# A hybrid decoder layer: the softmax values of one quad joined to the logits of a later quad, and retention's values of a head to the scores of the next

## The chip, the cores and the metric

The kernel runs on one core of a Trainium2 chip. The metric is the device time of one execution in microseconds (us), the median over the runs, lower is better. Four engines matter: TensorE (PE, matmuls; PEld is its weight loads), VectorE (DVE), ScalarE (ACT), and the DMA queues, mostly issued from SyncE (SP).

## What is computed

One layer on 256 tokens of width 2048, in fp32. The reference, cut to the middle part, which the change touches:

```python
x = x + 0.5 * gate1 * swiglu(modulate(rms_norm(x)), w_ffn1_gu, w_ffn1_down)
h = modulate(rms_norm(x))
rq, rk, rv, rg, sq, sk, sv, gl_ret, gl_swa = split(h @ w_in)
# sliding-window attention, 32 query heads over 8 key/value heads of 64, window 128, one sink per head
logits = einsum(q, k) * 64 ** -0.5              # masked to the window
probs = softmax(concat([logits, sink]))[..., :-1]
so = einsum(probs, v)
# retention, 8 heads: q, k of 128, v of 256, chunks of 128
scores = einsum(rotary(rq), rotary(rk)) * decay
ro = einsum(scores, rv) + (what comes over from the chunk before)
ro = silu(rg) * ro * rsqrt(mean(ro * ro) + 1e-6)
merged = sigmoid(gl_ret) * (ro @ w_ret_branch) + sigmoid(gl_swa) * (so @ w_swa_branch)
x = x + gate2 * (merged @ w_out)
x = x + 0.5 * gate3 * swiglu(modulate(rms_norm(x)), w_ffn2_gu, w_ffn2_down)
```

## The kernel before

**The large products.** Every weight is streamed from memory once, as tiles `raw` of 128 x 2048 (four row blocks by 512 columns). A tile is used in two **pieces** of 128 x 1024. For each piece ACT makes the high part `wh` (a cast to a shorter format, L351) and DVE makes the rest `wl = raw - wh` (L353). PE then does 12 matmuls of 512 columns: two row blocks, two halves of the tokens, and three products each (L338 and L339 with `wh`, L341 with `wl`). `wh` and `wl` come from a pool of three buffers each (`wsp`), so ACT can cast a piece only when PE has finished with the piece three before it.

**The work beside them.** The products of the projection `h @ w_in` come in chunks of 512 columns, each of 8 pieces: key and value of the attention, four chunks of its queries (SQ), four of retention's queries and keys (RQ, RK, with a rotation on DVE, L1262 to L1274), four of its values (RV), and so on. After every second piece `gemm` calls `step()`, which advances one generator of the list `side` by one yield. Softmax and retention run there, between the pieces. Rows of the conditioning matrix `w_ada` are summed on DVE as well (L206, four passes per row, at a pace set by `RATE_SOFT` and `RATE_AFTER`). The tile framework decides the order on PE, DVE and ACT from priorities and from its own picture of the timing; each engine then takes its list strictly in that order. SP's order is the order of the code.

**Softmax before.** A **quad** is four query heads that share one key head. `softmax_heads` runs quad g over four steps (parts 0 to 3) and beyond. Part 0, `quad_weights(g)`: a burst of logits on PE (8 matmuls, L1117, contraction of 64, so in 64 x 128 tiles of the array, into two `pd` and two `ps` banks); then on DVE the masked logits (L1125, four), the maximum (L1137, two), small operations (L1139 to L1141); on ACT eight exponentials (L1146); on DVE the sum, its inverse and the scaling (L1150 to L1153). Part 2: ACT takes the result apart into planes (L1167), a DMA of SP turns those of the quad before (L1176). Part 3 of the next quad: DVE puts the turned planes together into `turned_p` (L1188, four copies, `quad_together`). Part 1 two quads later: `quad_values`, a burst of 6 matmuls on PE (L1201, 128 x 64 tiles) into a `ps` bank of its own, copied out at L1205. Both bursts are placed with high priority behind the newest matmul of the big product.

**Retention before.** `retention(h)` makes the scores of head h (L1286, L1289), scales them by the decay on DVE, yields, then does the values (L1299 to L1301), their mean square (ACT) and the scaling, and yields again. A chunk of RV adds two heads to `side`.

Of the kernel before, what the change touches and what calls it, by code (L numbers as in the profile page):

```python
# [9 lines left out]
F32 = mybir.dt.float32  # L10
# [7 lines left out]
P = 128  # L18
S = 256
D = 2048  # L20
DFF = 5632
NT = S // P
# [8 lines left out]
RH, RDK, RDV = 8, 128, 256  # L31
QH, KVH, HD = 32, 8, 64
# [7 lines left out]
C_DEC = C_MASK + 3 * P  # L40
# [37 lines left out]
def layer_kernel(  # L78
# [56 lines left out]
    def a512():  # L135
        return t512()
# [177 lines left out]
    side = []  # L314
# [42 lines left out]
    cast, low, newest = [], [], []  # L357
# [173 lines left out]
    def flat_tile():  # L531

        return flat.tile([P, CH], F32, tag="flat", name=nm("flat"))
# [351 lines left out]
    part = [slot() for _ in range(3)]  # L885
# [212 lines left out]
    QUADS, HQ = QH // 4, 4  # L1098
# [6 lines left out]
    halves = [slice(i * HD, (i + 1) * HD) for i in range(2)]  # L1105
    asked, dec = set(), []

    def quad_weights(g):

        assert g // 2 in asked  # L1110
        late = [side_bank() for _ in range(2)]
        early_q = [bank() for _ in range(2)]
        with tc.issue_after(newest[-1]), tc.high_priority(offset=300):
            for ps, qs, n in ((late, slice(P, S), S), (early_q, slice(0, P), P)):
                for a in range(2):
                    for i, hs in enumerate(halves):
                        nc.tensor.matmul(  # L1117
                            ps[i][:, a * n : (a + 1) * n],
                            qo[hs, 2 * g + a, qs], skt[hs, g, :n], start=True, stop=True,
                        )  # L1120
        by_half = logits.rearrange("p (a i) n -> p a i n", a=2)
        for ps, ns in ((late, slice(P, W3)), (early_q, slice(0, P))):
            n = ns.stop - ns.start
            for i in range(2):
                nc.vector.scalar_tensor_tensor(  # L1125
                    out=by_half[:, :, i, ns],
                    in0=ps[i][:, : 2 * n].rearrange("p (a n) -> p a n", a=2),
                    scalar=HD**-0.5,
                    in1=mask[:, None, ns].broadcast_to([P, 2, n]),
                    op0=ALU.mult,  # L1130
                    op1=ALU.add,
                )
        mx, ng, se, sm = (small(2 * HQ, tag) for tag in ("mx", "ng", "se", "sm"))
        m2, n2, s2 = (v.rearrange("p (t i) -> p t i", t=2) for v in (mx, ng, se))
        parts_of = (logits[:, :, :P], logits[:, :, P:])
        for t, of_t in enumerate(parts_of):
            nc.vector.tensor_reduce(out=m2[:, t, :], in_=of_t, axis=AX.X, op=ALU.max)  # L1137
        sb = sink_b[:, HQ * g : HQ * (g + 1)][:, None, :].broadcast_to([P, 2, HQ])
        nc.vector.tensor_tensor(out=m2, in0=m2, in1=sb, op=ALU.max)  # L1139
        nc.vector.tensor_scalar(out=ng, in0=mx, scalar1=-1.0, scalar2=None, op0=ALU.mult)  # L1140
        nc.vector.tensor_tensor(out=s2, in0=n2, in1=sb, op=ALU.add)  # L1141
        nc.scalar.activation(se, se, AF.Exp)
        for t, of_t in enumerate(parts_of):
            for i in range(HQ):
                z = t * HQ + i
                nc.scalar.activation(  # L1146
                    of_t[:, i, :], of_t[:, i, :], AF.Exp,
                    bias=ng[:, z : z + 1], accum_out=sm[:, z : z + 1],
                )
        nc.vector.tensor_add(sm, sm, se)  # L1150
# [31 lines left out]
    def quad_together(turned):  # L1182

        for a in range(2):
            into = turned_p[:, 2 * a : 2 * a + 2].rearrange("p h b q -> p (h b q)")
            with tc.issue_after(low[-1]):
                for i in range(2):
                    nc.vector.tensor_copy(  # L1188
                        words(into)[:, :, i], turned[a][:, i * 2 * W3 : (i + 1) * 2 * W3]
                    )  # L1190

    def quad_values(g):

        po = bank()
        p4 = po.rearrange("p (a t q) -> p a t q", a=2, t=NT)
        vs = slice(g * HD, (g + 1) * HD)
        heads = turned_p.rearrange("p (a i) b q -> p a i b q", a=2)
        with tc.issue_after(newest[-1]), tc.high_priority(offset=300):
            for t, blk, tv in ((0, 0, 0), (1, 1, 0), (1, 2, 1)):
                for i in (1, 0):  # L1200
                    nc.tensor.matmul(  # L1201
                        p4[halves[i], :, t, :], sv[:, tv, vs], heads[:, :, i, blk, :],
                        start=blk < 2, stop=blk != 1,
                    )
        nc.any.tensor_copy(  # L1205
            qo[:, 2 * g : 2 * g + 2, :].rearrange("p a s -> p (a s)"), po
        )

    def softmax_heads():

        turned = {}
        for at in range(4 * (QUADS + 1) + 2):
            g, part = divmod(at, 4)
            if part == 0 and g < QUADS:
                quad_weights(g)
            if part == 1 and g >= 2:
                quad_values(g - 2)
            if part == 2 and g >= 1:
                turned[g - 1] = quad_turn()
            if part == 2 and g < QUADS:  # L1220
                quad_apart()
            if part == 3 and g >= 1:
                quad_together(turned.pop(g - 1))
                if g == QUADS:
                    dec.append(one.tile([P, D], F32, tag="row", name="dec"))
                    nc.gpsimd.dma_start(dec[0], consts[:, C_DEC:])
            yield
        pace["rate"] = RATE_AFTER
        turns.append(rows_beside())
# [19 lines left out]
    kept = set()  # L1249
# [30 lines left out]

    vo = slot().rearrange("p (t n) -> p t n", t=NT)

    def retention(h):
        assert {(0, h // 4), (1, h // 4)} <= kept
        ps = side_bank()
        nc.tensor.matmul(  # L1286
            ps[:, :S], qk[:, 1, h, :P], qk[:, 0, h, :], start=True, stop=True
        )
        nc.tensor.matmul(  # L1289
            ps[:, S : S + P], qk[:, 1, h, P:], qk[:, 0, h, P:], start=True, stop=True  # L1290
        )
        sc = a512()
        dh = dec[0][:, h * S : (h + 1) * S]
        nc.vector.tensor_mul(sc[:, :S], ps[:, :S], dh)
        nc.vector.tensor_mul(sc[:, S : S + P], ps[:, S : S + P], dh[:, :P])
        yield
        hv = slice(h * RDV, (h + 1) * RDV)
        po = side_bank()
        nc.tensor.matmul(po[:, :RDV], sc[:, :P], vo[:, 0, hv], start=True, stop=True)  # L1299
        nc.tensor.matmul(po[:, RDV:], sc[:, P:S], vo[:, 0, hv], start=True, stop=False)  # L1300
        nc.tensor.matmul(  # L1301
            po[:, RDV:], sc[:, S : S + P], vo[:, 1, hv], start=False, stop=True
        )
        v = small(NT, "rvar")
        junk = a512()
# [19 lines left out]
        yield  # L1325

    for ci in range(4):
        b = in_chunk(O_RV + ci * CH)
        for t in range(NT):
            nc.any.tensor_copy(vo[:, t, ci * CH : (ci + 1) * CH], b[t])  # L1330
        side += [retention(h) for h in (2 * ci, 2 * ci + 1)]

    def gates(p):

# [171 lines left out]
```

## Time and profile before

| what | value |
|---|---|
| median of 3 runs | 2375.23 us (2373.46 to 2377.26) |
| profiled execution | 2376.93 us, of which its span, first to last instruction, is 2375.2 us |
| granted TensorE clock | 0.998 |
| DVE busy | 1702.5 us (72%) |
| ACT busy | 1322.7 us (56%) |
| idle time of PE's matmuls put down to another engine between 880 and 1220 us, where softmax and retention run | 0.7 us |

Softmax begins at 882 us (first logits burst) and its last values burst ends at 1114 us; retention ends at 1209 us. Read a timeline row as: start, length, engine, line, operation, output<-inputs, shape, count, and in brackets the idle time before it with what ended it. Matmuls overlap in the pipeline, so the step from start to start is what one costs, not its length.

### The profile page before, as it was taken

The numbers are of one execution on the slowest core, as the hardware profiler recorded it, in microseconds if no ns is written. First come the engines' busy times: TensorE is split into PE (matmuls) and PEld (weight loads), VectorE is DVE, ScalarE is ACT, GpSimd is POOL, SyncE is SP. The second block draws the span as 40 slices with busy tenths as digits, with TensorE's granted clock in tenths as the row PEclk, the third lists the DMA queues.
The fourth block names the chain that finished last, engine by engine and source line by source line (L and its number), as shares of the span: only waits on it lengthen the run. The fifth ranks groups of instructions, "written<-read, shape, count | busy, mean of one in ns | idle before, by whom it ended". The sixth has DMA issues, their size and how long they took to land.

```text
span 2375.2 us, 28320 instructions
## 1 busy us (share of the span) xinstructions
PE 2342.6 (99%) x10438; PEld 1921.9 (81%) x10438; DVE 1702.5 (72%) x2635; ACT 1322.7 (56%) x1816; POOL 7.7 (0%) x18
## 2 busy tenths in 40 slices
PE   7999999999999999999999999999999999999998
PEld 5788888888788887778888888887888888888886
DVE  6887799788977768976777776677555555555656
ACT  6543456555446568775556564466445455455544
POOL 0000000000000000000000000000000000000000
PEclk9999999999999999999999999999999999999999
DMA  9977789998876787986778887755677777766553
GB/s 358 362 279 274 269 279 355 373 343 315 313 264 242 272 276 237 245 241 237 273 259 298 298 301 279 286 200 184 244 242 240 253 241 254 247 220 204 190 200 124
DMA packets 186028, 627.87 MB, mean 264 GB/s; under 512 B 108769, under 2 KB 109153, under 8 KB 115361
## 3 DMA queue, kind: packets, MB, share of 16 engines
q1 hardware_dynamic: 183810, 615.21, 74.4%
q0 software_dynamic: 1504, 9.81, 1.0%
q8 instruction: 82, 1.34, 0.2%
q10 hardware_dynamic: 576, 1.05, 0.1%
q14 instruction: 56, 0.46, 0.1%
HBM read 597.16 MB, written 4.22 MB: 253 GB/s over the span
## 4 chain that ended last, share of the span: by engine, by line
PE 94%; DVE 2%; DMA 2%; issue 1%; ACT 0%; SPq 0%; DVEq 0%; ACTq 0%
PE pa L341 31%; PE pa L338 31%; PE pa L339 31%; DMA raw<-in_w_ada_dram 1%; DVE wl L353 1%; PE ps L1201 0%; DMA x_sb<-in_x_dram 0%; DVE raw L206 0%; PE pd L1117 0%; DMA raw<-in_w_ffn_gu_dram 0%; DVE slot L206 0%; ACT wh L351 0%; PE ps L817 0%; DVE t L607 0%; PE ps L1117 0%
## 5 line engine op out<-in xcount | busy, mean ns | idle before, releaser
L353 DVE TENSOR_TENSOR wl<-raw,wh 128x1024 fp32r<-128x1024 f32 x794 | 964.6, 1222 | 532.9 <-ACT wh L351 531.1
L351 ACT CAST wh<-raw 128x1024 fp32r<-128x1024 f32 x794 | 833.5, 1053 | 906.1 <-PE pa L339 876.2
L338 PE MATMUL pa<-wh,hh 128*128 128x512 f32 x2192 | 856.4, 392 | 3.3 <-ACT wh L351 3.3
L339 PE MATMUL pa<-wh,hl 128*128 128x512 f32 x2192 | 855.2, 390 | 0.2 <-DVE hl L601 0.2
L341 PE MATMUL pa<-wl,hh 128*128 128x512 f32 x2192 | 779.4, 392 | 1.4 <-DVE wl L353 1.2
L338 PEld LDWEIGHTS pa<-wh,hh 128*128 128x128 f32 x2192 | 411.9, 188 | 92.3 <-ACT wh L351 5.3
L341 PEld LDWEIGHTS pa<-wl,hh 128*128 128x128 f32 x2192 | 410.5, 188 | 90.0 <-DVE wl L353 4.1
L339 PEld LDWEIGHTS pa<-wh,hl 128*128 128x128 f32 x2192 | 412.3, 188 | 85.2 <-DVE hl L601 0.4
L339 PE MATMUL pa<-wh,a 128*128 128x512 f32 x944 | 367.3, 391 | 0.0
L341 PE MATMUL pa<-wl,a 128*128 128x512 f32 x944 | 349.6, 391 | 3.1 <-DVE wl L353 3.1
L338 PE MATMUL pa<-wh,a 128*128 128x512 f32 x944 | 350.6, 391 | 0.0
L206 DVE CUSTOM_DVE_ANT_0 slot<-slot,cact 128x512 f32<-128x512 f32 (+1 forms) x280 | 210.3, 800 | 12.5 <-DMA slot<-in_w_ada_dram 12.5
L341 PEld LDWEIGHTS pa<-wl,a 128*128 128x128 f32 x944 | 177.7, 188 | 40.7 <-DVE wl L353 4.2
L339 PEld LDWEIGHTS pa<-wh,a 128*128 128x128 f32 x944 | 177.6, 188 | 38.4 <-DVE a L387 1.5
L338 PEld LDWEIGHTS pa<-wh,a 128*128 128x128 f32 x944 | 177.6, 188 | 37.0 <-ACT a L386 0.4
L512 ACT COPY slot<-back 128x512 uint16<-128x512 uint16 x140 | 93.4, 766 | 0.0
L206 DVE CUSTOM_DVE_ANT_0 raw<-raw,cact 128x512 f32<-128x512 f32 (+1 forms) x108 | 70.7, 706 | 21.2 <-DMA raw<-in_w_ada_dram 14.9
L206 DVE CUSTOM_DVE_ANT_0 rows_x<-rows_x,cact 128x512 f32<-128x512 f32 x124 | 78.7, 687 | 9.7 <-DMA rows_x<-in_w_ada_dram 9.3
L387 DVE TENSOR_TENSOR a<-slot,a 128x512 fp32r<-128x512 f32 x118 | 80.6, 684 | 0.3
L496 ACT COPY flat<-t 128x512 uint16<-128x512 uint16 x128 | 72.7, 617 | 3.0 <-DVE t L1274 2.6
L386 ACT CAST a<-slot 128x512 fp32r<-128x512 f32 x118 | 72.6, 616 | 0.0
L206 DVE DVE_READ_ACCUMULATOR2_ANT sums<- 128x1 f32 x512 | 42.0, 82 | 0.0
(206 smaller groups left out, 1162.5 us busy)
## 6 DMA issues: line engine op xcount, KB each, us to landing
raw<-in_w_ffn_gu_dram SPq DMA_DIRECT2D x160, 1024.0 KB, 5.2
raw<-in_w_in_dram SPq DMA_DIRECT2D x104, 1024.0 KB, 5.5
raw<-in_w_ffn_down_dram SPq DMA_DIRECT2D x88, 1024.0 KB, 4.8
slot<-in_w_ada_dram SPq DMA_DIRECT2D x83, 1024.0 KB, 7.2
rows_x<-in_w_ada_dram SPq DMA_DIRECT2D x31, 1024.0 KB, 7.4
raw<-in_w_ada_dram SPq DMA_DIRECT2D x26, 1024.0 KB, 5.5
raw<-in_w_ffn_gu_dram SPq DMA_DIRECT2D x32, 512.0 KB, 5.8
raw<-in_w_swa_branch_dram SPq DMA_DIRECT2D x16, 1024.0 KB, 6.0
```

The source lines that it names most:

```text
L206: nc.vector.tensor_tensor_reduce(out=w[:, at], in0=w[:, at], in1=cact[:, at], scale=1.0, scalar=0.0, op0=ALU.mult, op1=ALU.add, accum_out= ...
L338: nc.tensor.matmul(ps, ah[:, j, ts], wh[:, j, :], start=first, stop=False)
L339: nc.tensor.matmul(ps, al[:, j, ts], wh[:, j, :], start=False, stop=False)
L341: nc.tensor.matmul(ps, ah[:, j, ts], wl[:, j, :], start=False, stop=last).ins
L351: cast.append(nc.scalar.copy(hi, src).ins)
L353: low.append(nc.vector.tensor_sub(lo, src, hi.bitcast(F32)).ins)
L386: nc.scalar.copy(hi, v)
L387: nc.vector.tensor_sub(lo, v, hi.bitcast(F32))
L496: nc.scalar.copy(planes[:, i, :], words(src)[:, :, i])
L512: nc.scalar.copy(into[:, :, :, i], held["turned"][:, i])
```

## The change

**Softmax.** The logits of quad g and the values of quad g-3 go into one burst, `quad_burst`, at part 0: first the values, then the logits. The values no longer have a bank of their own: they go into the upper halves of the two `ps` banks whose lower halves take the early logits. They are copied out by two copies in place of one. `quad_together(g-2)` moves from part 3 of a quad to part 1 of the next, that is behind the burst. The generator is three steps longer; `dec`, retention's decay, is loaded one step earlier.

**Retention.** One generator for all heads: the values of head h-1 and the scores of head h in one burst, placed behind the newest matmul with high priority; nine steps in place of sixteen. The values go to a `ps` bank and not to a `pd` bank, the squares' unread output to a `flat` tile.

```diff
-    def quad_weights(g):
-        assert g // 2 in asked
-        late = [side_bank() for _ in range(2)]
-        early_q = [bank() for _ in range(2)]
+    def quad_burst(g, gv):
+        late = [side_bank() for _ in range(2)] if g is not None else None
+        both = [bank() for _ in range(2)]
         with tc.issue_after(newest[-1]), tc.high_priority(offset=300):
...
+            if gv is not None:
+                vs = slice(gv * HD, (gv + 1) * HD)
+                heads = turned_p.rearrange("p (a i) b q -> p a i b q", a=2)
+                for t, blk, tv in ((0, 0, 0), (1, 1, 0), (1, 2, 1)):
+                    for i in (1, 0):
                         nc.tensor.matmul(
+                            both[t][halves[i], S:].rearrange("p (a q) -> p a q", a=2),
+                            sv[:, tv, vs], heads[:, :, i, blk, :],
+                            start=blk < 2, stop=blk != 1,
                         )
+            if g is not None:
...
+                for ps, qs, n in ((late, slice(P, S), S), (both, slice(0, P), P)):
...
+        if gv is not None:
+            for t in range(NT):
+                nc.any.tensor_copy(
+                    qo[:, 2 * gv : 2 * gv + 2, t * P : (t + 1) * P],
+                    both[t][:, S:].rearrange("p (a q) -> p a q", a=2),
+                )
+        if g is not None:
+            quad_weights(g, late, both)
...
-        for at in range(4 * (QUADS + 1) + 2):
+        for at in range(4 * (QUADS + 2) + 1):
             g, part = divmod(at, 4)
-            if part == 0 and g < QUADS:
-                quad_weights(g)
-            if part == 1 and g >= 2:
-                quad_values(g - 2)
-            if part == 2 and g >= 1:
+            if part == 1 and 2 <= g < QUADS + 2:
+                quad_together(turned.pop(g - 2))
+            if part == 0 and (g < QUADS or g >= 3):
+                quad_burst(g if g < QUADS else None, g - 3 if g >= 3 else None)
+            if part == 2 and 1 <= g <= QUADS:
                 turned[g - 1] = quad_turn()
...
-            if part == 3 and g >= 1:
-                quad_together(turned.pop(g - 1))
...
     def retention(h):
-        assert {(0, h // 4), (1, h // 4)} <= kept
-        ps = side_bank()
...
+        g = h if h < RH else None
+        ps, po = side_bank(), bank()
+        with tc.issue_after(newest[-1]), tc.high_priority(offset=300):
+            if h > 0:
+                sc, hv = held_scores.pop(h - 1), slice((h - 1) * RDV, h * RDV)
+                nc.tensor.matmul(po[:, :RDV], sc[:, :P], vo[:, 0, hv], start=True, stop=True)
...
+            if g is not None:
+                assert {(0, h // 4), (1, h // 4)} <= kept
+                nc.tensor.matmul(
+                    ps[:, :S], qk[:, 1, h, :P], qk[:, 0, h, :], start=True, stop=True
+                )
...
+    def retention_heads():
+        for h in range(RH + 1):
+            while h // 2 not in valued and h < RH:
+                yield
+            retention(h)
+            yield
```

How the order moves is shown for quad 3 (its logits are the fourth burst of softmax), whose place in the program is the same in both kernels. Numbers behind a name are buffers and differ between the two programs. On PE, before, the logits of quad 3 stand alone, and the values of quad 1 follow three pieces and more later (not among these rows):

```order
L1117 MATMUL pd_7555<-slot_6204,slot_6366 128x256
L1117 MATMUL pd_7556<-slot_6204,slot_6366 128x256
L1117 MATMUL pd_7555<-slot_6204,slot_6366 128x256
L1117 MATMUL pd_7556<-slot_6204,slot_6366 128x256
L1117 MATMUL ps_7557<-slot_6204,slot_6366 128x128
```

and now the values of quad 0 stand right ahead of them (`soft` holds `turned_p`):

```order
L1118 MATMUL ps_7545<-soft,slot_6204 64x256 x2
L1118 MATMUL ps_7546<-soft,slot_6204 64x256 x4
L1128 MATMUL pd_7543<-slot_6204,slot_6366 128x256
L1128 MATMUL pd_7544<-slot_6204,slot_6366 128x256
L1128 MATMUL pd_7543<-slot_6204,slot_6366 128x256
```

Between this burst and the next PE has 96 matmuls of the big product, 8 pieces, with nothing between them; before, a values burst stood among the 96.

On ACT, before, at quad 3, from the cast of the third piece behind the burst (`wh_7642`) on:

```order
L351 CAST wh_7642<-raw_7640 128x1024
L496 COPY flat_7552<-t_7497 128x512 x2
L496 COPY flat_7629<-t_7504 128x512 x2
L351 CAST wh_7661<-raw_7640 128x1024
L351 CAST wh_7689<-raw_7687 128x1024
L351 CAST wh_7705<-raw_7687 128x1024
L1205 COPY slot_6366<-ps_7632 128x512
L1146 ACTIVATE soft,sm_7574<-soft,ng_7572 128x128 x4
L1146 ACTIVATE soft,sm_7574<-soft,ng_7572 128x256 x4
L1142 ACTIVATE se_7573<-se_7573 128x8
L351 CAST wh_7743<-raw_7741 128x1024
L351 CAST wh_7760<-raw_7741 128x1024
```

and now, again from the third piece on (`wh_7634`; L1134 copies the values out, L1168 is the exponentials):

```order
L351 CAST wh_7634<-raw_7632 128x1024
L496 COPY flat_7540<-t_7485 128x512 x2
L496 COPY flat_7625<-t_7492 128x512 x2
L1134 COPY slot_6366<-ps_7545 128x2x128
L1134 COPY slot_6366<-ps_7546 128x2x128
L351 CAST wh_7653<-raw_7632 128x1024
L1168 ACTIVATE soft,sm_7570<-soft,ng_7568 128x128 x3
L1164 ACTIVATE se_7569<-se_7569 128x8
L1168 ACTIVATE soft,sm_7570<-soft,ng_7568 128x128
L1168 ACTIVATE soft,sm_7570<-soft,ng_7568 128x256 x4
L351 CAST wh_7681<-raw_7679 128x1024
L351 CAST wh_7697<-raw_7679 128x1024
```

The exponentials stood behind the cast of the sixth piece after the burst; they stand behind that of the fourth now. Counted in the same way, quad 2 goes from five to four, and quads 2 to 7 all have four in the changed kernel, as quad 0 has in both.

On DVE, before, at quad 3, from the `wl` of the third piece on:

```order
L353 TENSOR_TENSOR wl_7643<-raw_7640,wh_7642 128x1024
L1125 SCALAR_TENSOR_TENSOR soft<-pd_7555,small_c 128x2x256
L1125 SCALAR_TENSOR_TENSOR soft<-pd_7556,small_c 128x2x256
L1125 SCALAR_TENSOR_TENSOR soft<-ps_7557,small_c 128x2x128
L1125 SCALAR_TENSOR_TENSOR soft<-ps_7558,small_c 128x2x128
L353 TENSOR_TENSOR wl_7662<-raw_7640,wh_7661 128x1024
L1137 TENSOR_REDUCE mx_7571<-soft 128x4 x2
L353 TENSOR_TENSOR wl_7690<-raw_7687,wh_7689 128x1024
L1139 TENSOR_TENSOR mx_7571<-mx_7571,sink_b 128x8
L353 TENSOR_TENSOR wl_7706<-raw_7687,wh_7705 128x1024
L1140 TENSOR_SCALAR ng_7572<-mx_7571 128x8
```

and now (L1210 is `quad_together`, L1147 the masked logits, L1159 the maximum, L1162 `ng`, on which the exponentials wait, L1172 the sum, which waits for them):

```order
L353 TENSOR_TENSOR wl_7635<-raw_7632,wh_7634 128x1024
L1210 COPY soft<-a_7443 128x768 x2
L1210 COPY soft<-a_7444 128x768 x2
L1147 SCALAR_TENSOR_TENSOR soft<-pd_7543,small_c 128x2x256
L1147 SCALAR_TENSOR_TENSOR soft<-pd_7544,small_c 128x2x256
L1147 SCALAR_TENSOR_TENSOR soft<-ps_7545,small_c 128x2x128
L353 TENSOR_TENSOR wl_7654<-raw_7632,wh_7653 128x1024
L1159 TENSOR_REDUCE mx_7567<-soft 128x4 x2
L1161 TENSOR_TENSOR mx_7567<-mx_7567,sink_b 128x8
L1162 TENSOR_SCALAR ng_7568<-mx_7567 128x8
L1163 TENSOR_TENSOR se_7569<-ng_7568,sink_b 128x8
L1172 TENSOR_TENSOR sm_7570<-sm_7570,se_7569 128x8
```

The copies of `quad_together` have come in ahead of the masked logits, and no `wl` stands any more between the maximum and the sum.

More of the change, by code (lines that the diff above doesn't have):

```diff
@@ L1190, in quad_together @@
                     )
[L1192 to L1207, printed above, removed]
     def softmax_heads():
         turned = {}
-        for at in range(4 * (QUADS + 1) + 2):
+        for at in range(4 * (QUADS + 2) + 1):
             g, part = divmod(at, 4)
-            if part == 0 and g < QUADS:
-                quad_weights(g)
-            if part == 1 and g >= 2:
-                quad_values(g - 2)
-            if part == 2 and g >= 1:
+            if part == 1 and 2 <= g < QUADS + 2:
[3 more added lines that the diff above has]
+            if part == 2 and 1 <= g <= QUADS:
                 turned[g - 1] = quad_turn()
@@ L1221, in softmax_heads @@
                 quad_apart()
-            if part == 3 and g >= 1:
-                quad_together(turned.pop(g - 1))
-                if g == QUADS:
-                    dec.append(one.tile([P, D], F32, tag="row", name="dec"))
-                    nc.gpsimd.dma_start(dec[0], consts[:, C_DEC:])
+            if part == 2 and g == QUADS:
+                dec.append(one.tile([P, D], F32, tag="row", name="dec"))
+                nc.gpsimd.dma_start(dec[0], consts[:, C_DEC:])
             yield
@@ L1281, in layer_kernel @@
     vo = slot().rearrange("p (t n) -> p t n", t=NT)
+    held_scores = {}
     def retention(h):
-        assert {(0, h // 4), (1, h // 4)} <= kept
-        ps = side_bank()
[L1286 to L1303, printed above, removed]
+        g = h if h < RH else None
+        ps, po = side_bank(), bank()
@@ new lines, in retention @@
+        with tc.issue_after(newest[-1]), tc.high_priority(offset=300):
+            if h > 0:
+                sc, hv = held_scores.pop(h - 1), slice((h - 1) * RDV, h * RDV)
+                nc.tensor.matmul(po[:, :RDV], sc[:, :P], vo[:, 0, hv], start=True, stop=True)
+                nc.tensor.matmul(
+                    po[:, RDV:], sc[:, P:S], vo[:, 0, hv], start=True, stop=False
+                )
+                nc.tensor.matmul(
+                    po[:, RDV:], sc[:, S : S + P], vo[:, 1, hv], start=False, stop=True
+                )
+            if g is not None:
+                assert {(0, h // 4), (1, h // 4)} <= kept
+                nc.tensor.matmul(
+                    ps[:, :S], qk[:, 1, h, :P], qk[:, 0, h, :], start=True, stop=True
+                )
+                nc.tensor.matmul(
+                    ps[:, S : S + P], qk[:, 1, h, P:], qk[:, 0, h, P:], start=True, stop=True
+                )
@@ L1304, in retention @@
+        if g is not None:
+            sc = held_scores[h] = a512()
+            dh = dec[0][:, h * S : (h + 1) * S]
+            nc.vector.tensor_mul(sc[:, :S], ps[:, :S], dh)
+            nc.vector.tensor_mul(sc[:, S : S + P], ps[:, S : S + P], dh[:, :P])
+        if h == 0:
+            return
         v = small(NT, "rvar")
-        junk = a512()
+        junk = flat_tile()
         for t in range(NT):
@@ L1324, in retention @@
             )
-        yield
+    def retention_heads():
[4 more added lines that the diff above has]
+            yield
+    valued = set()
+    side.append(retention_heads())
     for ci in range(4):
@@ L1330, in layer_kernel @@
             nc.any.tensor_copy(vo[:, t, ci * CH : (ci + 1) * CH], b[t])
-        side += [retention(h) for h in (2 * ci, 2 * ci + 1)]
+        valued.add(ci)
     def gates(p):
```

11 lines of the change are left out of this document (6 added, 5 removed).

## The prediction

> **What bounds the kernel now.** I read the page first: the busy times of the engines (busy time, share, instructions) and the shares of the chain of waits.
>
> ```profile
> PE 2342.6 (99%) x10438; PEld 1921.9 (81%) x10438; DVE 1702.5 (72%) x2635; ACT 1322.7 (56%) x1816; POOL 7.7 (0%) x18
> PE 94%; DVE 2%; DMA 2%; issue 1%; ACT 0%; SPq 0%; DVEq 0%; ACTq 0%
> ```
>
> PE has work for the whole span, so a change can gain only what it takes out of PE's own time, and loses whatever it makes PE wait. Then the waits of PE between 880 and 1220 us, the stretch that the change touches (total, times, longest):
>
> ```profile
> PE pa L338 <- ACT wh L351: 0.5, 1, 0.5
> PE pa L341 <- DVE wl L353: 0.2, 1, 0.2
> ```
>
> Two waits, 0.7 us: softmax and retention are hidden already, and there is next to no stall to win. How near the two other engines are to becoming a stall, the groups of instructions from 880 to 1130 us tell (busy, mean ns | idle before them and its cause):
>
> ```profile
> L353 DVE TENSOR_TENSOR wl<-raw,wh 128x1024 fp32r<-128x1024 f32 x81 | 97.7, 1220 | 30.4 <-ACT wh L351 29.7 <-PE pd L1117 0.8
> L351 ACT CAST wh<-raw 128x1024 fp32r<-128x1024 f32 x81 | 83.9, 1050 | 56.0 <-PE pa L339 48.9 <-DMA raw<-in_w_in_dram 4.3 <-issue 2.2
> L1150 DVE TENSOR_TENSOR sm<-sm,se 128x8 f32<-128x8 f32 x8 | 1.3, 166 | 17.8 <-ACT se L1142 10.0 <-ACT soft L1146 7.8
> ```
>
> ACT's casts mostly wait for PE to free a `wh` buffer (48.9 us over 81 pieces): the normal state, in which ACT is three pieces ahead. The pieces live on that lead. The row of L1150 matters too: DVE stands 17.8 us, 2.2 us a quad, for the exponentials, and whatever is queued behind the sum stands with it.
>
> **The change, part by part. What the joint bursts save.** The logits of quad 3 and the values of quad 1 in PE's timeline:
>
> ```profile
> 954.66 0.39 PE L341 MATMUL pa<-wl,hh 128*128 128x512 f32 x1
> 954.97 1.14 PE L1117 MATMUL pd<-slot,slot 64*128 64x256 f32 x8
> 955.94 0.61 PE L1117 MATMUL ps<-slot,slot 64*128 64x128 f32 x8
> 956.48 0.50 PE L338 MATMUL pa<-wh,hh 128*128 128x512 f32 x1
> 956.82 0.39 PE L339 MATMUL pa<-wh,hl 128*128 128x512 f32 x1
> ```
>
> ```profile
> 965.23 0.39 PE L338 MATMUL pa<-wh,hh 128*128 128x512 f32 x1
> 965.55 1.52 PE L1201 MATMUL ps<-soft,slot 128*64 128x256 f32 x12
> 966.99 0.50 PE L341 MATMUL pa<-wl,hh 128*128 128x512 f32 x1
> 967.33 0.39 PE L339 MATMUL pa<-wh,hl 128*128 128x512 f32 x1
> ```
>
> and retention's scores, in full tiles:
>
> ```profile
> 1070.39 0.59 PE L1286 MATMUL pd<-slot 128*128 128x256 f32 x2
> 1070.82 0.38 PE L1289 MATMUL pd<-slot 128*128 128x128 f32 x2
> 1070.96 0.47 PE L338 MATMUL pa<-wh,hh 128*128 128x512 f32 x1
> 1071.27 0.39 PE L339 MATMUL pa<-wh,hl 128*128 128x512 f32 x1
> ```
>
> A matmul of the big product costs 0.227 us from start to start (quad 0 below: 51 steps from 883.54 to 895.24 are 11.70 us, of which the step right behind a burst is 0.11 longer, as 956.48 to 956.82 is), a pass of 256 columns 0.215 us (1070.39 to 1070.82, two passes). From 1070.39 to 1071.27 are 0.88 us, and 2 x 0.215 + 2 x 0.108 + 0.227 are 0.87: a burst of full tiles has no cost at its ends. So retention's joint burst saves nothing, and its matmuls are the same. The logits take 2.16 us from 954.66 to 956.82; less two big matmuls, 1.71. Their passes, two half tiles side by side, are 8 x 0.215 / 2 + 8 x 0.108 / 2 = 1.29, so the two ends cost 0.42. The values in the same way: 2.10 - 0.45 = 1.65, less 12 x 0.215 / 2 = 1.29, so 0.36. An end is some 0.2 us. In a joint burst one end of each goes (0.39), and a switch from values to logits, which no row of before shows, comes in: between 0 and the 0.2 of any other switch of tile form. I take 0.2, since the two forms (128 x 64 and 64 x 128) differ as much as either does from the full tile. Five joint bursts (quads 3 to 7) save 5 x 0.2 = **1.0 us**, at most 2.0. [...]
>
> **What the new order costs.** In quads 2 to 7 the exponentials now stand on ACT right behind the cast of the fourth piece after the burst, ahead of the fifth. Quad 0 already has this order, so it is the template. On PE, ACT and DVE:
>
> ```profile
> 883.54 0.50 PE L338 MATMUL pa<-wh,hh 128*128 128x512 f32 x1
> ...
> 895.24 0.39 PE L339 MATMUL pa<-wh,hl 128*128 128x512 f32 x1
> 896.10 0.50 PE L338 MATMUL pa<-wh,hh 128*128 128x512 f32 x1 [0.48 <-ACT wh L351]
> ```
>
> ```profile
> 886.37 1.06 ACT L351 CAST wh<-raw 128x1024 fp32r<-128x1024 f32 x1 [3.16 <-PE pa L339]
> ...
> 889.50 0.40 ACT L1146 ACTIVATE soft<-soft,ng 128x128 f32<-128x128 f32 x1 [0.77 <-DVE ng L1140]
> ...
> 893.13 2.93 ACT L351 CAST wh<-raw 128x1024 fp32r<-128x1024 f32 x3
> ```
>
> ```profile
> 883.24 1.22 DVE L353 TENSOR_TENSOR wl<-raw,wh 128x1024 fp32r<-128x1024 f32 x1 [0.76 <-PE pd L1117]
> 884.38 1.28 DVE L1125 SCALAR_TENSOR_TENSOR soft<-pd,small_c 128x512 f32<-128x512 f32 x2
> ...
> 886.24 1.80 DVE L1137 TENSOR_REDUCE mx<-soft 128x4 f32<-128x1024 f32 x2
> 888.08 0.17 DVE L1139 TENSOR_TENSOR mx<-mx,sink_b 128x8 f32<-128x8 f32 x1
> 888.16 1.22 DVE L353 TENSOR_TENSOR wl<-raw,wh 128x1024 fp32r<-128x1024 f32 x1
> 889.30 0.17 DVE L1140 TENSOR_SCALAR ng<-mx 128x8 f32<-128x8 f32 x1
> ```
>
> Call t the first big matmul behind the burst, 883.54. ACT casts the fourth piece from t+2.83, waits for `ng`, and does the exponentials from 889.50 to 893.13, 3.63 us. Three casts follow, done 2.93 later, at t+12.5. PE wanted the third of them at 895.24 + 0.23 = t+11.93 and got it 0.63 us late. So the exponentials must end by t+9.0, and each microsecond after that is a microsecond of PE. Quad 0 ended them at t+9.6. What differs in quads 2 to 7:
>
> *Copies ahead.* `quad_together` stands on DVE between the third `wl` and the masked logits: 1.97 us (945.28 to 947.25 below). In joint bursts, about 3 us long, the third cast starts with the burst, its `wl` is done some 0.8 us before t (-3 + 1.05 + 1.2), the copies at t+1.2, the masked logits (1.86, from 884.38 to 886.24) at t+3.05, against t+2.7 in quad 0. In quads 4, 6 and 7 the rest is as in quad 0: exponentials to t+10.0, **1.0 us of stall each, 3.0**.
>
> *The fourth `wl` ahead of the maximum* (quads 2, 3, 5): it waits for the fourth cast, t+2.83 + 1.05, and ends near t+5.0; maximum 1.84, small operations 0.3, `ng` at t+7.2, exponentials to t+10.9. **Quad 2: 1.95 us.**
>
> *A backlog on DVE* (quads 3, 5), from the rotation and the rows of `w_ada`:
>
> ```profile
> 941.96 0.17 DVE L1150 TENSOR_TENSOR sm<-sm,se 128x8 f32<-128x8 f32 x1 [2.55 <-ACT se L1142]
> ...
> 945.28 2.06 DVE L1188 COPY soft<-a 128x768 uint16<-128x768 uint16 x4
> 947.25 1.20 DVE L353 TENSOR_TENSOR wl<-raw,wh 128x1024 fp32r<-128x1024 f32 x1
> ...
> 959.85 1.28 DVE L1125 SCALAR_TENSOR_TENSOR soft<-pd,small_c 128x512 f32<-128x512 f32 x2
> ```
>
> From the sum of quad 2 to the masked logits of quad 3 DVE works 17.9 us with one gap of 0.5; in the new order it has one `wl` more between them, 19.0. From one t to the next are 8 pieces of 2.72 us, a burst of 3 and quad 2's own stall, 26.8; the sum comes at t+11.0. That leaves 15.8 us until the next t: the masked logits begin at t+3.2 and not at t+1.2 and end at t+5.05, the fourth `wl` ends at t+6.2 and not at t+5.0, and the exponentials at t+12.1. **3.15 us each, 6.3.**
>
> The sum of waits is 3.0 + 1.95 + 6.3 = 11.25 us. That the copying out of the values (now two copies, L1134) must end before DVE reads the early logits in the same bank I take at nothing: they stand ahead of the fourth cast, in ACT's 3.16 us of idle above. Without that cover it is at most 0.7 us a burst, 3.5. The wait of 0.2 for `wl`, for a late load, moves with the order: I count it as gone. Later loading of `dec` and later passes over `w_ada` end long before they are used; nothing.
>
> Sum: 11.25 - 1.0 - 0.2 = 10.05 us more. The profiled execution, 2376.93 us, would be 2387.0; it lies 1.7 above the median of the runs, so the median goes from 2375.23 to **2385.3 us**.
>
> **Rivals.** *The exponentials stay covered (not slower).* If `ng` comes by t+5.2, they end by t+8.9 and no piece is late; then only 1.2 us of gain is left: 2374.0. For it: DVE is idle 30 us ahead of its `wl` (the row of L353), so it may be ready earlier than quad 0 was. Against it: quad 0, without copies and backlog, was late already.
>
> *Only DVE's throughput counts.* The windows (length, then busy of PE, PEld, DVE, ACT) show how full it is:
>
> ```profile
> 930.00:955.00 25.00, 25.00 (x126) 19.77 (x124) 21.80 (x40) 19.02 (x38) 0.00 (x0) 1.00 0.82 235
> 955.00:980.00 25.00, 25.00 (x125) 19.93 (x124) 22.85 (x42) 19.12 (x38) 0.00 (x0) 1.00 0.75 203
> 980.00:1005.00 25.00, 25.00 (x124) 19.96 (x124) 21.46 (x38) 20.13 (x39) 0.00 (x0) 1.00 1.08 283
> ```
>
> With no `wl` left between maximum and sum, DVE idles 3.63 us a quad; 21.80 + 3.63 is 0.4 over 25, 22.85 + 3.63 is 1.5 over, 21.46 + 3.63 is 0.1 over. If a queue of that length is all that it takes, PE loses 2.0 us, less 1.2: 2376.0, no change. Against it: a stall comes from the lead of three pieces, not from an average.
>
> *All six quads behave like quad 3 (slower still).* It decides if the first delay leaves DVE a backlog that the next quad inherits: 6 x 3.15 - 1.2 = 17.7, so 2392.9. Against it: half of the quads carry no rotation.
>
> **How the numbers follow.** Forecast 0.65, covered 0.12, throughput only 0.13, all six 0.10. The time is the forecast's, 2385.3; its own range is 2379 (the two backlogged quads no worse than quad 2, a free switch, quads 4, 6, 7 at 0.2) to 2390 (the bank's 3.5 and a little more). The range reaches down to the throughput case and up to near the last: 2375.5 to 2391.5. A difference below 0.2% (4.75 us) can't be told from none. Slower takes most of the forecast and the last case; same, the throughput case, most of the covered one and a small part of the forecast; faster would need 4.75 us, which no wait of PE before can yield: slower 0.72, same 0.23, faster 0.05.
>
> **What the changed profile would show.** PE waiting for `wh` (L351) in each of quads 2 to 7, some 12 us behind the burst, 1 to 3 us, largest in quads 3 and 5; ACT waiting for `ng` behind the fourth cast; joint bursts of about 3 us; no change at retention's bursts. It is wrong if PE's waits between 900 and 1120 stay below 2 us, or if they come from `wl` and not from `wh`.

## The result, and the profile after

| | median | runs | profiled execution | its span | granted clock |
|---|---|---|---|---|---|
| before | 2376.14 us | 2373.46 to 2377.26 (4) | 2376.93 us | 2375.2 us | 0.998 |
| changed | 2399.89 us | 2397.63 to 2402.95 (4) | 2401.99 us | 2400.2 us | 0.995 |

The changed kernel is slower: the ratio is 1.0099, with an interval of 1.0086 to 1.0111. The page of the changed kernel, busy times and chain of waits:

```profile
PE 2352.4 (98%) x10438; PEld 1925.1 (80%) x10438; DVE 1701.4 (71%) x2635; ACT 1322.1 (55%) x1822; POOL 7.7 (0%) x18
PE 92%; DVE 3%; DMA 2%; ACT 1%; issue 1%; SPq 0%; DVEq 0%; ACTq 0%
```

PE's busy time went up by 10 us though it does the same 10438 matmuls, and the rest of the 25 us is idle. So there are two things to find: waits, and matmuls that take longer. The waits of PE between 870 and 1260 us (total, times, longest):

```profile
PE pa L338 <- ACT wh L351: 15.2, 12, 2.5
```

Twelve waits for `wh`. One of them is quad 0's 0.5, the only one that stood there before; eleven are new. Quad 5 shows what happens; t, its first big matmul behind the joint burst, is 1018.87. PE's timeline:

```profile
1029.70 0.39 PE L341 MATMUL pa<-wl,hh 128*128 128x512 f32 x1
1032.42 0.51 PE L338 MATMUL pa<-wh,hh 128*128 128x512 f32 x1 [2.33 <-ACT wh L351]
...
1033.23 0.40 PE L339 MATMUL pa<-wh,hl 128*128 128x512 f32 x1
1034.40 0.79 PE L338 MATMUL pa<-wh,hh 128*128 128x512 f32 x1 [0.77 <-ACT wh L351]
1034.99 0.63 PE L339 MATMUL pa<-wh,hl 128*128 128x512 f32 x1
1035.42 0.63 PE L338 MATMUL pa<-wh,hh 128*128 128x512 f32 x1
```

PE stops at the fifth piece (2.72 from start to start, where 0.227 is normal), goes on, stops again for the last of the three casts, and then a matmul takes 0.43 and not 0.227. ACT in the same stretch, without the rows between:

```profile
1021.79 1.05 ACT L351 CAST wh<-raw 128x1024 fp32r<-128x1024 f32 x1 [1.73 <-PE pa L339]
1027.71 0.40 ACT L1168 ACTIVATE soft<-soft,ng 128x128 f32<-128x128 f32 x1 [4.86 <-DVE ng L1162]
...
1031.34 3.01 ACT L351 CAST wh<-raw 128x1024 fp32r<-128x1024 f32 x3
```

The fourth cast, 4.9 us of waiting for `ng`, the exponentials to t+12.5, then three casts in a row: quad 0's pattern, later. DVE says why `ng` is late (L1210 is `quad_together`, L1147 the masked logits):

```profile
1020.54 2.06 DVE L1210 COPY soft<-a 128x768 uint16<-128x768 uint16 x4
1022.48 1.27 DVE L1147 SCALAR_TENSOR_TENSOR soft<-pd,small_c 128x512 f32<-128x512 f32 x2
```

The same copies hold something else. SP's queue, with the transposes of `planes` into the two `a` buffers (L1198) and the weight loads (L328):

```profile
1021.70 3.28 SPq L1198 DMA_TRANSPOSE a<-planes_of  x2
1025.38 1.49 SPq L328 DMA_DIRECT2D raw<-in_w_in_dram  x3
```

In the kernel before, these stand at

```profile
997.58 5.67 SPq L1176 DMA_TRANSPOSE a<-planes_of  x2
1003.65 5.87 SPq L328 DMA_DIRECT2D raw<-in_w_in_dram  x3
```

that is 9.3 us ahead of that quad's t (1006.84) and 3.2 ahead, where now it is 2.8 and 6.5 behind. The waits of SP (900 to 1130 us) name the releaser, first of the changed kernel, then of the one before:

```profile
SPq L1198 <- DVE soft L1210: 104.8, 7, 21.7
```

```profile
SPq L1176 <- DVE soft L1188: 17.7, 5, 7.9
```

A transpose may write `a` only when the copies of `quad_together` have read what it held. They stood three steps ahead of the next quad's transposes in the code and stand one step ahead now, so SP stands up to 21.7 us at a transpose, with the loads of the weights queued behind it. (Before, SP's longest wait at a transpose was 11.8 us, for ACT's taking apart at L1167, and a single cast waited for a load, 4.3 us.) In quad 5 the first of these loads lands 5.4 us after its issue (the view of the tile `raw`), at 1030.8, which is t+11.9: half a microsecond before the exponentials end. So in this quad two chains reach the fifth cast at almost the same time. The windows over quad 5 (length, busy of PE, PEld, DVE, ACT, POOL, granted clock, DMA share, GB/s) show the starved loads and the clock:

```profile
1020.00:1025.00 5.00, 5.00 (x24) 4.11 (x23) 5.00 (x10) 1.12 (x2) 0.00 (x0) 1.00 0.48 91
...
1030.00:1035.00 5.00, 1.90 (x7) 1.18 (x7) 3.47 (x6) 5.00 (x11) 0.00 (x0) 0.87 1.00 392
1035.00:1040.00 5.00, 5.00 (x13) 3.94 (x12) 2.13 (x2) 2.79 (x5) 0.00 (x0) 0.50 1.12 304
```

Behind the waits PE is fully busy and does 13 matmuls in 5 us, not 22: the granted clock is 0.50. The matmuls of the changed kernel fall to this rate three times (behind quads 3, 5 and 7): 32 steps of 0.427 us and three of 0.59.

The last wait has only the loads as its cause: behind a values burst without logits, so without exponentials, ACT stands 6.85 us for a load:

```profile
1107.88 1.05 ACT L351 CAST wh<-raw 128x1024 fp32r<-128x1024 f32 x1 [2.35 <-PE pa L339]
1115.78 2.00 ACT L351 CAST wh<-raw 128x1024 fp32r<-128x1024 f32 x2 [6.85 <-DMA raw<-in_w_in_dram]
```

And the joint burst itself, on PE at quad 3:

```profile
957.61 0.39 PE L341 MATMUL pa<-wl,hh 128*128 128x512 f32 x1
957.93 1.52 PE L1118 MATMUL ps<-soft,slot 128*64 128x256 f32 x12
959.38 1.13 PE L1128 MATMUL pd<-slot,slot 64*128 64x256 f32 x8
960.34 0.61 PE L1128 MATMUL ps<-slot,slot 64*128 64x128 f32 x8
960.88 0.50 PE L338 MATMUL pa<-wh,hh 128*128 128x512 f32 x1
961.23 0.40 PE L339 MATMUL pa<-wh,hl 128*128 128x512 f32 x1
```

It takes 3.62 - 0.45 = 3.16 us, where the two bursts took 1.71 + 1.65 = 3.36.

### The profile page after: what moved, and what is told of

It reads as the page before. It is cut to its first block, busy times and chain, and to the rows that moved or that the text cites. A ratio compares the mean times of both kernels' runs of the same rounds, so it can differ in the third digit from the quotient of the medians.

```text
span 2400.2 us, 28339 instructions
## 1 busy us (share of the span) xinstructions
PE 2352.4 (98%) x10438; PEld 1925.1 (80%) x10438; DVE 1701.4 (71%) x2635; ACT 1322.1 (55%) x1822; POOL 7.7 (0%) x18
## 4 chain that ended last, share of the span: by engine, by line
PE 92%; DVE 3%; DMA 2%; ACT 1%; issue 1%; SPq 0%; DVEq 0%; ACTq 0%
PE pa L341 30%; PE pa L338 30%; PE pa L339 30%; DMA raw<-in_w_in_dram 1%; DMA raw<-in_w_ada_dram 1%; DVE wl L353 1%; ACT wh L351 1%; PE ps L1118 0%; ACT soft L1168 0%; DMA x_sb<-in_x_dram 0%; PE pd L1128 0%; DVE slot L206 0%; DVE raw L206 0%; DVE soft L1147 0%; DVE mx L1159 0%
## 5 line engine op out<-in xcount | busy, mean ns | idle before, releaser
L387 DVE TENSOR_TENSOR a<-slot,a 128x512 fp32r<-128x512 f32 x118 | 80.6, 684 | 0.3
```

Source lines behind the costliest of these rows:

```text
L387: nc.vector.tensor_sub(lo, v, hi.bitcast(F32))
```

## The experiments

Theory X is the prediction's: `ng` and the exponentials are late and stand ahead of the casts. Theory S is what the traces added: SP, held at the transposes, loads late. Ratios are against the kernel before on the same chip, with their intervals.

**Which part.** The two parts of the diff, each alone.

> The kernel before with the retention part of the change alone. Theory (all the loss is in softmax): retention's bursts are full tiles without a cost at their ends, so joining them costs and saves nothing; 2376 us, within 2 of the kernel before, and PE waits less than 1 us between 880 and 1260 us. Rival (the values in a ps bank, or retention queued behind one another, make PE or the banks wait): 2380 us or more, with waits of PE behind 1150 us.

Measured: 2375.65 us, ratio 0.9994 (0.9985 to 1.0002); the only wait of PE there is quad 0's 0.5. Retention neither costs nor gains.

> The softmax part of the change alone, retention as before. Theory: the whole loss, 2398 to 2403 us, with PE waiting for wh (L351) some 17 us in quads 2 to 7 and the granted clock at half in two or three stretches. Rival (retention has a share): below 2396 us.

Measured: 2400.55 us, ratio 1.0096 (1.0083 to 1.0110); waits for `wh` 15.3 us. The loss is all softmax's.

**The place of the exponentials alone.**

```diff
+    def quad_exp():
+        parts_of, se, ng, sm = held_exp.pop()
+        with tc.issue_after(cast[-1]):
+            nc.scalar.activation(se, se, AF.Exp)
...
+            if part == 3 and g < QUADS:
+                quad_exp()
-            if part == 2 and g < QUADS:
+            if part == 3 and g < QUADS:
                 quad_apart()
```

> The whole change, but the exponentials and what follows them are issued behind the sixth cast after the burst and not the fourth. Theory (the place of the exponentials in ACT's queue makes the loss): they end near t+12.8 in all quads, but the fifth and sixth casts are ahead of them, so PE waits less than 1.5 us in softmax, the clock stays at full, and the joint bursts' 1.0 us shows: 2374 to 2377 us. Rival (the joint burst, or DVE's load, makes the loss wherever the exponentials stand): 2385 us or more, with waits for wl or wh in quads 2 to 7.

Measured: 2399.06 us, ratio 1.0086 (1.0073 to 1.0100): neither the time of the first nor the waits of the second alone. In the profiled execution (2394.3 us, the lowest of the four) the fifth cast of quad 5 stands ahead of the exponentials and is late all the same; ACT's timeline:

```profile
1017.38 1.05 ACT L351 CAST wh<-raw 128x1024 fp32r<-128x1024 f32 x1 [1.28 <-PE pa L339]
1027.19 2.00 ACT L351 CAST wh<-raw 128x1024 fp32r<-128x1024 f32 x2 [8.75 <-DMA raw<-in_w_in_dram]
```

With the exponentials out of the way the load's landing shows, t+12.7 here. That was the row that led to SP and to theory S. DVE gave some of it back too: its sums wait for the exponentials, now later, with `wl` behind them (quad 4; L1180 is the sum):

```profile
1003.35 0.17 DVE L1180 TENSOR_TENSOR sm<-sm,se 128x8 f32<-128x8 f32 x1 [2.21 <-ACT soft L1176]
...
1005.53 1.22 DVE L353 TENSOR_TENSOR wl<-raw,wh 128x1024 fp32r<-128x1024 f32 x1
```

That part is the larger one: of PE's waits in this run (870 to 1260 us) more are for `wl` than for `wh`.

```profile
PE pa L341 <- DVE wl L353: 8.2, 8, 2.3
PE pa L338 <- ACT wh L351: 5.5, 6, 2.5
```

The late loads reach PE directly in the second row. The first row is mostly the sums, which wait for exponentials that now stand behind late casts; how much of it the place alone would cost, with the loads on time, no run shows.

**The clock.** `keep_warm` places matmuls of `hh` by itself, into a bank that nothing reads, behind the newest matmul.

```diff
+            if part == 2 and g in (2, 3, 5, 7):
+                keep_warm(10)
```

> The whole change, and ten matmuls into an unused bank, 2.3 us, right ahead of the fifth piece after the burst in quads 2, 3, 5 and 7, where PE waits 1.1 to 2.7 us. Theory (steps of 0.427 us come from a clock that is halved where PE has been idle too much): the matmuls fill the waits, the granted clock stays at 1.00 through softmax, the casts come when they came, and the time falls by the 7.5 us of slow steps, less up to 1.5 in quad 7: 2391 to 2395 us. Rival (the slow steps have another cause, a late load or the weights): they stay, 2399 us or more.

Measured: 2392.49 us, ratio 1.0059 (1.0044 to 1.0074), 7.4 us less than the changed kernel by the medians, 9.5 by the ratios (the two ran on different chips), and inside the theory's range. On PE and in the windows at quad 5:

```profile
1025.66 2.43 PE L1219 MATMUL pd<-hh 128*128 128x512 f32 x10
```

```profile
1025.00:1035.00 10.00, 8.97 (x39) 6.78 (x38) 6.37 (x8) 9.83 (x20) 0.00 (x0) 1.00 1.03 380
```

The casts come as late as they did (in quad 5 the exponentials still end at t+12.6), yet the clock stays at 1.00. The slow matmuls are a consequence of the waits and a cost of their own.

**Loads on time.** Only the place in the code of two steps is changed:

```diff
-            if part == 2 and 1 <= g <= QUADS:
+            if part == 3 and 1 <= g <= QUADS:
                 turned[g - 1] = quad_turn()
-            if part == 2 and g < QUADS:
+            if part == 3 and g < QUADS:
                 quad_apart()
```

> The whole change, but SP's transposes of quad g-1, and the taking apart of quad g ahead of them in ACT's queue, are issued one step (two pieces) later. Theory S (the loss starts on SP: the transposes wait for the two a buffers, which the moved copies of quad_together free later, and the weight loads queued behind them come late; the early place of the exponentials follows from it, since the framework plans them where the casts lack their data): SP is no longer held, the exponentials stand behind the fifth to seventh cast, PE waits less than 2 us in softmax: 2374 to 2379 us. Theory X (the loss is the lateness of ng and the exponentials: copies ahead of the masked logits and DVE's backlog, which are the same here): waits as in the run with the exponentials behind the sixth cast, 2390 us or more.

Measured: 2378.85 us, ratio 1.0010 (1.0001 to 1.0019). Nine tenths of the loss are gone, with the copies where the change put them. The framework now sets the exponentials behind the sixth or seventh cast in quads 2 to 7 by itself (the fourth in the changed kernel). The waits of SP and of PE:

```profile
SPq L1198 <- DVE soft L1210: 74.8, 7, 13.7
```

```profile
PE pa L341 <- DVE wl L353: 2.0, 4, 0.7
```

SP still waits long, but at a place where it is far enough ahead. The 2 us that are left are `wl` behind the sums.

The same with the changed kernel's order on ACT forced:

```diff
+            if part == 2 and 2 <= g < QUADS:
+                hold.append(last_exp[-1])
...
+        if hold:
+            with tc.issue_after(hold.pop()):
+                cast.append(nc.scalar.copy(hi, src).ins)
...
```

> As the run before (transposes one step later), with the fifth piece's cast held behind the exponentials in quads 2 to 7, so that ACT has the order of the changed kernel while the loads are on time. Theory X: exponentials end where they did, at t+10 to t+12.6, PE waits for wh by what this is over t+9.1, 12 to 17 us in all, and the clock may halve: 2389 to 2400 us. Theory S in its strong form (the order on ACT costs nothing by itself): 2374 to 2379 us. If both hold, each alone suffices.

Measured: 2394.32 us, ratio 1.0073 (1.0059 to 1.0086). ACT's waits, 900 to 1130 us, hold no load any more (L355 is the cast here, L1174 the exponentials):

```profile
ACT wh L355 <- PE pa L339: 40.3, 25, 2.4
ACT soft L1174 <- DVE ng L1167: 23.2, 6, 6.2
```

PE's waits are 13.2 us, and matmuls at half clock cost 5.9 more (the granted clock is 0.995 over the execution). So early exponentials suffice for most of the loss with the loads on time: 1.0073, against 1.0099 with both and 1.0010 with neither. Late loads without early exponentials were not measured by themselves: the 1.0086 of the run with the exponentials behind the sixth cast also holds the `wl` waits behind its sums.

**The copies later still**, a test in which the theories forecast opposite signs:

```diff
-            if part == 1 and 2 <= g < QUADS + 2:
+            if part == 2 and 2 <= g < QUADS + 2:
                 quad_together(turned.pop(g - 2))
```

> The whole change, but quad_together one step (two pieces) later, ahead of the transposes in the code. The copies leave their place ahead of the masked logits, so ng and the exponentials come 1 to 2 us earlier; SP's transposes wait up to two pieces longer for the a buffers. Theory S: the weight loads behind them are 4 to 5 us later in six or seven quads: 2415 to 2440 us, PE waiting for wh with ACT's casts waiting for DMA. Theory X: fewer waits, 2385 to 2396 us.

Measured: 2436.29 us, ratio 1.0251 (1.0237 to 1.0265), though the exponentials of quads 4, 6 and 7 end at t+7.8, 2 to 3 us earlier than in the changed kernel. PE waits 43.6 us for `wh` (870 to 1260 us), 0.5 of it in quad 0 and the rest in seven stops of 5.0 to 7.8 us, and the clock drops with them: it was 0.54 from 1015 to 1020 us, behind one of the stops, and 0.990 over the execution, against 0.995 in the changed kernel. The sign is theory S's; its path is only part of it. In quads 4, 6 and 7 the fifth cast waits for its load, to t+15.1 and later, where it began at t+9.9 to t+11.1 in the changed kernel. In quads 2, 3 and 5 no cast waits for a load: the casts follow on ACT's taking apart (L1189), which now stands ahead of them and waits for the transposes to have read `planes`, which I had not listed. ACT's waits (11.9 of the 20.1 us are one wait behind a values burst alone):

```profile
ACT wh L351 <- DMA raw<-in_w_in_dram: 20.1, 8, 11.9
...
ACT planes_of L1189 <- DMA a<-planes_of: 8.1, 6, 2.5
```

**ACT's order in the kernel before**, forced by the same `hold` and nothing else:

> The kernel before, with nothing changed but the fifth piece's cast held behind the exponentials in quads 2 to 7. Theory X: where a backlog makes the exponentials late (quads 3 and 5, near t+14) PE waits 3 to 4 us each, elsewhere the separate values burst covers it; 2381 to 2388 us, with half clock 2 to 5 more. Theory S: the loads are on time, so within 2 us of the kernel before, 2374 to 2379 us.

Measured: 2381.89 us, ratio 1.0023 (1.0013 to 1.0033), at the low end of X's. PE waits 2.3 and 1.6 us in quads 3 and 5, 0.5 in quad 2, nothing in the others, where there are no copies ahead of the masked logits and the values burst gives ACT time.

**Joint bursts with the copies at their old place.**

```diff
-            if part == 1 and 2 <= g < QUADS + 2:
-                quad_together(turned.pop(g - 2))
...
-                quad_burst(g if g < QUADS else None, g - 3 if g >= 3 else None)
...
+                quad_burst(g if g < QUADS else None, g - 2 if g >= 2 else None)
...
+            if part == 3 and 1 <= g <= QUADS:
+                quad_together(turned.pop(g - 1))
```

> The joint bursts kept, but quad_together back at part 3, where the kernel before has it, and so the values of quad g-2 (not g-3) with the logits of quad g. Theory S and X together (the moved copies are the cause, not the joint burst): SP waits for the a buffers no longer than before, the copies do not stand ahead of the masked logits; the framework puts the exponentials behind the fourth to sixth cast, and where it is the fourth they end near t+9.7 to t+10.2 without a values burst as cover, 0.6 to 1.1 us of wait each in four quads; no half clock; 2376 to 2381 us. Rival (a joint burst delays ACT and DVE by itself): 2385 us or more.

Measured: 2383.04 us, ratio 1.0024 (1.0013 to 1.0036), above the range, but not for its reason: between 900 and 1260 us PE waits for nothing. The exponentials behind the fourth cast end between t+7.8 and t+9.3, in time for the t+9.0 of the template or close to it. PE's waits from 1260 to 1500 us show the rest:

```profile
PE pa L339 <- DVE a L387: 3.3, 2, 1.7
```

A `w_ada` pass waits there for its load ahead of the split of an operand. Softmax was one step shorter than before, so the faster pace began earlier.

> As the run with the copies as before, with softmax one step longer, as many steps as in the kernel before, so that the faster pace of the w_ada rows begins at the same piece. Theory (the 5 us that the run before it lost behind softmax, at 1299 to 1313 us, are a row's pass on DVE that waits for its load ahead of the operands' split at L387, moved there by the earlier pace): these waits go, the softmax stage stays without waits, six joint bursts save 1.2 us: 2374 to 2378 us. Rival (retention's shorter list of steps moves the passes, not softmax's length): the waits near 1300 stay, 2380 to 2385 us.

Measured: 2375.98 us, ratio 0.9997 (0.9988 to 1.0006); of the waits for L387 0.3 us is left. With retention as before:

> As the run before, with retention as in the kernel before, so that only softmax's joint bursts differ from it. Theory: no waits of PE between 900 and 1260 us beyond those of before, six joint bursts save 1.2 us: 2374 to 2378 us, which a measurement can hardly tell from before. Rival (the joint burst costs somewhere else): 2380 us or more.

Measured: 2376.99 us, ratio 1.0000 (0.9991 to 1.0008). Six joint bursts, 1.2 us, are too little to be told from no change; but nothing is lost either. The joint burst was never the cost.

**The backlog.** Five operations of the rotation (L1265 to L1277 now) replaced by a copy. This kernel leaves the rotation out, so it does not compute the layer and serves for the time alone:

> The whole change, with the rotation of retention's queries and keys left out (one copy in place of five operations of DVE per tile). Theory (in quads 2, 3 and 5 DVE's backlog makes the copies late, and with them both the loads and the exponentials): these quads become like 4 and 6, exponentials to about t+10, 1.4 us of wait each, no half clock in them: 2383 to 2389 us. Rival (the copies' place alone decides, the backlog is nothing): 2397 us or more.

Measured: 2390.38 us, ratio 1.0056 (1.0042 to 1.0069), a little above the theory's range. The exponentials end at t+10.7 and t+10.9 in quads 3 and 5 (12.6 in the changed kernel) and at t+12.0 in quad 2 (12.7); the granted clock is 0.998 over the execution, as in the kernel before (0.995 in the changed kernel). The backlog is a share of the lateness in 3 and 5, little of it in quad 2.

## Why the prediction was right or wrong

The direction and the place were right, the size was not: 10 us were forecast, 23.75 came. The terms, in the profiled executions (waits as steps from start to start less 0.227):

| term | forecast | measured |
|---|---|---|
| five joint bursts | -1.0 | 5 x (3.16 - 3.36) = -1.0 |
| the wait at 1050 us | -0.2 | -0.35 |
| waits in quads 2 / 3 / 4 / 5 / 6 / 7 | 1.95 / 3.15 / 1.0 / 3.15 / 1.0 / 1.0 = 11.25 | 3.5 / 3.3 / 1.4 / 3.4 / 1.4 / 2.6 = 15.7 |
| wait behind a values burst alone | 0 | 1.0 |
| the first step behind ten waits at full clock, 0.11 longer | 0 | 1.1 |
| matmuls at half clock, with the first steps behind three waits | 0 | 32 x 0.20 + 3 x 0.36 = 7.5 |
| ahead of softmax, not of the change | 0 | 0.85 |
| sum | 10.05 | 24.8 |

The two profiled executions differ by 25.1 us; 0.3 of it is in none of these terms.

*The bursts* were sized right to a tenth, and so was retention: nothing (first run). *The template* held, and with it the forecast's mechanism: in the run with the transposes later and ACT's order forced no cast waits for a load, and PE's waits are 13.2 us, against 11.25. The exponentials end at t+10.0 and t+9.9 in quads 4 and 6 (forecast t+10.0), at t+12.6 in 3 and 5 (forecast t+12.1), and PE loses about what they are past t+9 (3.3 and 3.4 us in quads 3 and 5); in quads 4, 6 and 7 it loses 0.4 to 0.8 us more, where the third of the three casts waits another 0.40 to 0.49 us for its load. At t+9.3 it loses nothing (the run with the copies at their old place).

*The step that failed first* is "Copies ahead": it priced the moved `quad_together` by its 1.97 us on DVE and asked only who stands behind it there. Its copies also release the two `a` buffers to SP's transposes, where SP now waits up to 21.7 us, and the weight loads stand behind those. The prediction had SP's queue in none of its terms. Because the late loads reach the fifth cast together with the late exponentials, the miss is worth less than either chain: with the loads on time and ACT's order kept (the forced run) the time is 2394.3 us, 5.6 below the changed kernel by the medians, 6.2 by the ratios, and the two intervals only touch. But the late loads are a second cause of the loss, and they are the whole of the 1.0 us behind the burst of values alone. That the planner puts the exponentials early because the casts' data is late in its own picture fits the run with the transposes later, whose exponentials went back; shown is only that the one change of place moved both.

*The largest missing term* is the clock, 7.5 us, half of the 15 by which the sum is short: a wait was priced at its own length, and what PE does afterwards at its normal pace. With the waits filled the clock was 1.00 in the windows at quads 2, 3 and 5 and 0.998 over the execution, and the time fell by about as much.

*Mis-sized terms:* quad 2 was reckoned as a joint burst without backlog, but it has logits alone, and its copies begin at t+0.7, not before t; 3.5 us and not 1.95. Quad 7's exponentials ended at t+10.8, not t+10.0.

*The rivals.* "Covered" and "only DVE's throughput" fell: the waits are 15.7 us, where they allowed 0 and 2.0. "All six like quad 3" was nearer in time (2392.9) but not in kind; quads 4 and 6 stayed short.

## What to carry to other kernels

Ask of a moved read which buffer it releases, who waits for this buffer, and what is queued behind that: here four copies of 0.5 us held a DMA queue for up to 21.7 us. Keep the distance between the reader of a buffer and its next writer when steps are put in another order; one step more of it, with the order that the framework then chose on ACT, took 21 us of the loss away. Where an engine that is always busy comes to wait, price the wait and then the clock behind it: here 15.7 us of waits in quads 2 to 7 had 7.5 us of slower steps behind them.

## What the runs showed of the hardware

In the changed kernel's softmax stage the granted clock was 0.50 three times: from 975.71 us for 6.83 us, from 1033.73 for 6.83 and from 1091.76 for 3.41, in the waits of quads 3, 5 and 7 and behind them. It was also 0.50 for 3.41 us from 648.03, far ahead of the change. Quad 2 (940 to 950), quad 3 (970 to 985) and quad 7 (1088 to 1096) in windows (length, busy of PE, PEld, DVE, ACT, POOL, granted clock, DMA share, GB/s):

```profile
940.00:950.00 10.00, 6.79 (x29) 5.00 (x28) 6.25 (x12) 8.87 (x24) 0.00 (x0) 1.00 1.02 380
...
970.00:975.00 5.00, 2.67 (x12) 1.89 (x11) 1.46 (x4) 5.00 (x19) 0.00 (x0) 1.00 1.01 418
975.00:980.00 5.00, 4.32 (x12) 3.09 (x11) 4.15 (x4) 4.21 (x6) 0.00 (x0) 0.57 1.07 329
980.00:985.00 5.00, 5.00 (x18) 3.99 (x17) 1.93 (x3) 3.58 (x6) 0.00 (x0) 0.75 0.42 131
...
1088.00:1091.00 3.00, 1.60 (x6) 0.67 (x4) 2.93 (x5) 2.24 (x3) 0.00 (x0) 1.00 1.02 431
1091.00:1096.00 5.00, 4.14 (x11) 3.32 (x12) 2.66 (x3) 3.74 (x5) 0.00 (x0) 0.66 0.73 310
```

In this execution the length of the waits does not tell by itself where the clock falls: quad 2 waits as long as quad 3 (3.5 and 3.3 us) and stays at 1.00, and quad 7 waits less (2.6 us) and falls. What decides is not shown. The clock goes with the spread of the times: the changed kernel's runs at a mean clock of 0.995 took 2401.99 and 2402.95 us, those at 0.997 took 2397.63 and 2397.80.
